# Keys and probabilities in one tile that starts its data 112 bytes up

## The chip, the cores and the metric

The kernel runs on one core of a Trainium2 chip. The metric is the device time of one execution in microseconds (us). Before the change the median of three runs is 1506.08 us (1505.47 to 1506.26). One more execution was profiled; the traces quoted below are of that one.

## The reference

One encoder layer on a sequence of 256 tokens of width 4096, all in float32: a LayerNorm, one wide input projection (4096 to 13,312 columns), two branches that read it, and one output projection with a residual and a second LayerNorm.

```python
p = x @ w_in
y_conv = c_b * centred_short_conv(c_c * c_h, conv_w) * silu(c_z)      # 2048 channels
y_attn = banded_window_attention(a_q, a_k, a_v, sink) * silu(a_z)     # 16 query heads, 4 kv heads, dim 128
y = concatenate([y_conv, y_attn]) @ w_out
return layer_norm(DN_ALPHA * x + y, ln_g, ln_b)
```

The attention of one head takes queries times keys, adds a bias by distance (and masks beyond 128 tokens), makes probabilities with a sink logit in the denominator, and multiplies them with the values.

## The kernel before, in words

Nearly all time is in the two projections. Their weights stream in from memory in pieces of 128 x 2048, and each piece is split into a rounded half `whi` (ScalarE, L204) and a remainder `wlo` (VectorE, L208), so that TensorE can multiply in a reduced float32 form (`F32R`) and still keep float32 accuracy: activations high and low times `whi`, activations high times `wlo`. In a matmul the activations `xT` (or sums of them, `SC`) are the stationary operand, 128 columns; 256 columns of `whi` or `wlo` are the moving operand. Some steps are "pairs" (L257 to L279), which save multiplications by a 7-product scheme, others are plain (L236 to L253, and L909 to L924 for the output projection).

The order of work is written by hand (a manual schedule). A loop (L805 to L829) issues one weight step after another; other work is hung on step numbers with `at(step, function, ...)` and is issued after the step's matmuls on the engines' queues. The input chunks come in the order keys, values, then four times (gate, queries) for the four groups of four heads, then the convolution's chunks. When a group's queries are done, `SPREAD` (L631 to L633) hangs the work of its four heads on the following 32 steps:

- `q_tr`, `q_lo` (L546 to L554): transpose queries into `qhl`, high and low.
- `scores` (L556 to L565): six matmuls, stationary `qhl`, moving `kT` (256 columns). They come at steps 8, 9, 13 and 21 of a group.
- `s_add`, `exps`, `recip`, `norms`: softmax on VectorE and ScalarE.
- `p_tr` (L599 to L607): four transposes of the probabilities on TensorE (128 columns each, at steps 13, 19, 24 and 28), and ScalarE writes the high half of `pT` from their result; `p_lo` (L609) has VectorE write the low half.
- `pv` (L613 to L620): six matmuls, stationary `v`, moving `pT` (256 columns), at steps 19, 22, 28 and 31.
- `out_z` (L622): times the gate, and a store to memory.

So at step 13 the transposes of the first head stand right ahead of the scores of the third, and at steps 19 and 28 a `pv` stands right ahead of the next head's transposes; the other bursts of six have weight matmuls on both sides. Each head has one `scores` and one `pv`: 32 bursts of six in the whole kernel.

`kT` holds the keys of two groups at a time; the keys of the other two are parked in memory through the tile `klate` (which has the place of `pT`, L513) and loaded back by `k_load` (L526) one group later. `v` and `vlate` do the same in the place of `qhl`.

Tiles of a pool lie one after another in each partition, in the order in which they are first named. These are the bytes at which the data of the tiles start, and the remainder by 128:

| tile | role in its matmuls | starts at byte | remainder by 128 |
|---|---|---|---|
| `whi` (3 buffers), `wlo0` to `wlo2` | moving | 82,928; 91,376; 99,824; 132,848; 141,296; 149,744 | 112 |
| `w0`, `w1`, `w2` | moving, in the last step alone | 108,256; 116,448; 124,640 | 96 |
| `kT` | moving | 190,080 | 0 |
| `pT` | moving | 208,512 | 0 |
| `xT` | stationary | 17,280 | 0 |
| `SC` | stationary | 158,336 | 0 |
| `v` | stationary | 194,176 | 0 |
| `qhl` | stationary | 220,800 | 0 |

`whi` and `wlo` have 16 unused bytes ahead of their data (`OFF`, L51, used in `half_tile`, L193 to L200). The last weight step takes its two halves out of the raw buffers `w0` to `w2` instead (L198 to L200), without those 16 bytes; the matmuls that read them are L923 like the others of the output projection.

The pool `pa` holds all attention tiles; when the last head is done it is closed and the pool `pc` opens over the same bytes (`open_pc`, L635).

Of the kernel before, what the change touches and what calls it, by code (L numbers as in the profile page):

```python
# [8 lines left out]
F32 = mybir.dt.float32  # L9
F32R = mybir.dt.float32r  # L10
# [4 lines left out]
P = 128  # L15
D = 4096
S = 256
# [32 lines left out]
N_W = 3  # L50
OFF = 4  # L51
GAP = 64


def units(ci):
# [45 lines left out]
def encoder_kernel(ctx: ExitStack, tc: tile.TileContext, x, emb_g, emb_b, wi, ws, conv_w, sink, wo, ln_g, ln_b, out):  # L101
# [91 lines left out]
    def half_tile(j, name):  # L193
        if j < len(steps) - 1 and name == "whi":
            return wpool.tile([P, PIECE + GAP], F32R, name=name)[:, OFF:OFF + PIECE]
        if j < len(steps) - 1:
# [32 lines left out]
    for name in ("whi", "w0", "w1", "w2", "wlo0", "m", "nm", "wlo1", "den", "es", "wlo2"):  # L229
        n = {"whi": PIECE + GAP}.get(name, PIECE + 2 * OFF if name[:3] == "wlo" else PIECE if name[0] == "w" else 2)  # L230
        wpool.tile([P, n], F32, name=name, bufs={"whi": 3, "m": 4, "nm": 3, "den": 4, "es": 3}.get(name, 1))
# [61 lines left out]
    with tc.tile_pool(name="pro", bufs=1) as pro:  # L293
# [7 lines left out]
        def x_load(i, *cols):  # L301
            for c0, c1 in zip(cols, cols[1:]):
                nc.sync.dma_start(out=xs[i][:, c0:c1], in_=x[i * P:(i + 1) * P, c0:c1])
# [4 lines left out]

        first = [wpool.tile([P, PIECE + GAP], F32, name=f"first{j}", tag="whi")[:, OFF:OFF + PIECE] for j in range(2)]
        x_load(0, 0, 1024, 2048, 3072, 3584, 3840, 4096)  # L310
# [158 lines left out]
    pa = ph.enter_context(tc.tile_pool(name="pa", bufs=1))  # L469
# [15 lines left out]
    def turned(t):  # L485

        return [turned_bank(t, b) for b in range(2)]
# [8 lines left out]
    def halves(hi, lo, src):  # L496
        nc.scalar.activation(hi, src, AF.Copy)
        nc.vector.tensor_tensor(lo, src, hi.bitcast(F32), op=ALU.subtract)

    st_ = {}  # L500
    kT = pa.tile([P, 2, 2, S], F32R, name="kT")
    v = pa.tile([P, 2, 2, 2, P], F32R, name="v")
    kd = dram.tile([P, 2, 2, S], F32, name="kd")
    vd = dram.tile([P, 2, 2, 2, P], F32, name="vd")
# [5 lines left out]

    def k_turn(g):

        late = pa.tile([P, 2, 2, S], F32R, name="klate", tag="pT")  # L513
        for t, ps in zip((kT, late), turned(st_.pop("k"))):
            halves(t[:, :, 0, :], t[:, :, 1, :], ps)
        nc.sync.dma_start(out=kd, in_=late.bitcast(F32))
# [82 lines left out]
    def p_tr(h):  # L599
        p = st_.pop(("p", h))[0]  # L600
        t_ps = ps_att.tile([P, 2, S], F32, name="att")
        for kb in range(2):
            for b in range(2):
                nc.tensor.transpose(t_ps[:, kb, b * P:(b + 1) * P], p[:, b, kb * P:(kb + 1) * P], ident)  # L604
        t = pa.tile([P, 2, 2, S], F32R, name="pT")
        nc.scalar.activation(t[:, 0, :, :], t_ps, AF.Copy)
        st_["pT", h] = t, t_ps  # L607

# [19 lines left out]
    def head(n, *steps):  # L628
        return [(t, f, n) for t, f in zip(steps, (scores, s_add, exps, recip, norms, p_tr, p_lo, pv, out_z))]
# [135 lines left out]
    def chunk_end(j, ci):  # L765
        c0, fn = next((c, f) for c, f in ENDS if IN_ORDER[ci] >= c)
        g = IN_ORDER[ci] - c0
        fn(ci, g)
        if fn is end_k:
            at(j + 1, k_turn, g)  # L770
        if fn is end_cz:
            at(j + 5, s_act)
        if fn is end_z:
            at(j + 5, z_act)
            for b in range(2):
                at(j + 11 + 2 * b, z_tr, g, b) if g else at(j + 8 + b, z_tr, g, b)
        if fn is end_q:
            h = g * GROUP
            for t, f, a in SPREAD:
                at(j + t, f, a if f in (q_tr, q_lo) else h + a)  # L780
            if g < 2:
                at(j + 22, k_load, g)
                at(j + 32, v_load, g)
        if fn in (end_ch, end_cb):
            key, other, tr, mul = ("u", "c", conv_tr, conv_mul) if fn is end_ch else ("g", "s", gate_tr, gate_mul)
            last = ci == len(IN_ORDER) - 1
            if last:
                product(key, other)
            else:
                at(j + (8 if ci == c_ch0 else 4), product, key, other)  # L790
            for t, f, b in ((2, tr, 0), (2, tr, 1), (3, mul, 0), (3, mul, 1)) if last else (
                    (10, tr, 0), (11, tr, 1), (18, mul, 0), (21, mul, 1)) if ci == c_ch0 else (
                            (6, tr, 0), (7, tr, 1), (7, mul, 0), (9, mul, 1)):
                at(j + t, f, g, b)
# [340 lines left out]
```

## Time and profile before

| | |
|---|---|
| median of 3 runs | 1506.08 us |
| the profiled execution's own time | 1505.99 us |
| its span, first to last instruction | 1504.3 us |
| TensorE matmuls busy | 1490.8 us, 99% |
| VectorE busy | 1329.7 us, 88% |
| ScalarE busy | 781.7 us, 52% |
| mean granted TensorE clock | 0.999 |

A busy time is the union of an engine's instructions. Matmuls overlap: each lasts some 0.28 us from start to end, and the next one starts about 0.11 us after it, so the pace of TensorE is read from start to start (or from a long busy stretch divided by its count), not from the length of one.

### The profile page before, as it was taken

The page shows a single profiled execution, that of the slowest core. Times are in us where ns is not written, and L with a number is a line of the kernel's source. Part 1 is how long each engine was busy: PE and PEld are TensorE (multiplying, and loading weights), DVE is VectorE, ACT ScalarE, POOL GpSimd, SP SyncE. Part 2 cuts the span into 40 slices and gives each one's busy share as a digit, 9 for nine tenths or more (in the row PEclk, how much of TensorE's full clock was granted, in tenths as well). Part 3 has the DMA queues.
Part 4 walks back from the last instruction along what each step waited for, and adds up shares of the span by engine and source line. Part 5 has one row for each costly group of instructions (what it writes and reads, how often), then busy time and mean ns, then how long its engine had stood idle before and what let it go on. Part 6 is the DMA issues. An engine that isn't in the chain of part 4 may idle for free.

```text
span 1504.3 us, 30113 instructions
## 1 busy us (share of the span) xinstructions
PE 1490.8 (99%) x12947; PEld 1475.4 (98%) x12947; DVE 1329.7 (88%) x1555; ACT 781.7 (52%) x669; POOL 1.3 (0%) x7
## 2 busy tenths in 40 slices
PE   7999999999999999999999999999999999999998
PEld 4999999999999999999999999999999999999997
DVE  7768989999899998999899999999899688888876
ACT  4545556656566665545555455544556444444431
POOL 0000000000000000000000000000000000000000
PEclk9999999999999999999999999999999999999999
DMA  7555555656555555656556655656557656766673
GB/s 289 217 182 197 210 197 170 208 183 207 196 186 190 181 186 206 233 197 238 187 195 218 220 197 196 220 184 227 205 206 297 261 204 219 261 217 217 219 261 123
DMA packets 71749, 316.18 MB, mean 210 GB/s; under 512 B 8544, under 2 KB 12608, under 8 KB 50880
## 3 DMA queue, kind: packets, MB, share of 16 engines
q1 hardware_dynamic: 70608, 312.43, 58.7%
q8 instruction: 101, 1.65, 0.4%
q10 hardware_dynamic: 1008, 1.84, 0.3%
q14 instruction: 32, 0.26, 0.1%
HBM read 305.23 MB, written 8.91 MB: 209 GB/s over the span
## 4 chain that ended last, share of the span: by engine, by line
PE 98%; DVE 1%; DMA 0%; ACT 0%; SPq 0%; issue 0%; ACTq 0%
PE acc L251 45%; PE acc L923 20%; PE pacc L276 6%; PE pacc L277 6%; PE pacc L279 6%; PE acc L277 4%; PE acc L276 4%; PE acc L279 4%; PE att L493 1%; PE att L618 1%; DVE st L330 0%; PE att L604 0%; PE acc L380 0%; DMA x<-in_x 0%; PE att L363 0%; DVE x L338 0%
## 5 line engine op out<-in xcount | busy, mean ns | idle before, releaser
L204 ACT ACTIVATE whi<-w 128x2048 fp32r<-128x2048 f32 (+1 forms) x354 | 621.7, 1761 | 593.8 <-DVE w L185 231.0
L208 DVE TENSOR_TENSOR wlo<-w,whi 128x2048 fp32r<-128x2048 f32 (+1 forms) x354 | 736.1, 2083 | 102.7 <-ACT whi L204 83.6
L251 PE MATMUL acc<-whi,xT 128*128 128x256 f32 x3952 | 474.0, 276 | 0.0
L251 PEld LDWEIGHTS acc<-whi,xT 128*128 128x128 f32 x3952 | 459.9, 188 | 0.0
L251 PE MATMUL acc<-wlo,xT 128*128 128x256 f32 x1976 | 245.8, 275 | 0.0
L251 PEld LDWEIGHTS acc<-wlo,xT 128*128 128x128 f32 x1976 | 234.0, 188 | 0.0
L923 PE MATMUL acc<-whi,xT 128*128 128x256 f32 x1696 | 201.8, 275 | 0.0
L923 PEld LDWEIGHTS acc<-whi,xT 128*128 128x128 f32 x1696 | 196.6, 188 | 0.4 <-issue 0.4
L183 DVE TENSOR_TENSOR w<-w 128x512 f32<-128x512 f32 x179 | 122.4, 684 | 8.3 <-DMA w<-in_ws 8.3
L923 PE MATMUL acc<-wlo,xT 128*128 128x256 f32 x848 | 105.3, 275 | 0.0
L276 PE MATMUL acc<-whi,xT 128*128 128x256 f32 x370 | 102.1, 276 | 0.0
L277 PE MATMUL acc<-whi,xT 128*128 128x256 f32 x370 | 102.1, 276 | 0.0
L923 PEld LDWEIGHTS acc<-wlo,xT 128*128 128x128 f32 x848 | 100.4, 188 | 0.0
L276 PE MATMUL pacc<-whi,xT 128*128 128x256 f32 x350 | 98.2, 281 | 0.0
L277 PE MATMUL pacc<-whi,xT 128*128 128x256 f32 x350 | 96.5, 276 | 0.0
L279 PE MATMUL pacc<-wlo,xT 128*128 128x256 f32 x350 | 96.2, 275 | 0.0
L279 PE MATMUL acc<-wlo,xT 128*128 128x256 f32 x370 | 92.8, 275 | 0.0
L277 PE MATMUL pacc<-whi,SC 128*128 128x256 f32 x330 | 91.0, 276 | 0.0
L276 PE MATMUL pacc<-whi,SC 128*128 128x256 f32 x330 | 91.0, 276 | 0.0
L279 PE MATMUL pacc<-wlo,SC 128*128 128x256 f32 x330 | 82.9, 275 | 0.0
L184 DVE TENSOR_TENSOR w<-w 128x256 f32<-128x256 f32 x179 | 76.1, 425 | 6.2
L185 DVE TENSOR_TENSOR w<-w 128x256 f32<-128x256 f32 x179 | 76.1, 425 | 6.2
(220 smaller groups left out, 1674.3 us busy)
## 6 DMA issues: line engine op xcount, KB each, us to landing
w<-in_wi SPq DMA_DIRECT2D x112, 1024.0 KB
w<-in_ws SPq DMA_DIRECT2D x202, 512.0 KB
w<-in_wo SPq DMA_DIRECT2D x41, 1024.0 KB
R<-in_wo SPq DMA_DIRECT2D x13, 1024.0 KB
x<-in_x SPq DMA_DIRECT2D x7, 512.0 KB
yl<-yd SPq DMA_DIRECT2D x7, 512.0 KB
xc<-in_x SPq DMA_DIRECT2D x14, 256.0 KB
R<-in_ws SPq DMA_DIRECT2D x6, 512.0 KB
```

The lines of the kernel that those rows point to most:

```text
L183: nc.vector.tensor_tensor(s01, b22, b12.to_broadcast([P, 2, HW]), op=ALU.add)
L184: nc.vector.tensor_tensor(r(6), r(5), r(1), op=ALU.add)
L185: nc.vector.tensor_tensor(r(7), r(6), r(3), op=ALU.add)
L204: nc.scalar.activation(part(j, wh[j]), part(j, raw[j]), AF.Copy)
L208: nc.vector.tensor_tensor(part(j, wl[j]), part(j, raw[j]), part(j, wh[j]).bitcast(F32), op=ALU.subtract)
L251: nc.tensor.matmul(acc[ci, i][:, c:c + HW], x, w[:, k * W + c:k * W + c + HW], start=(first and w is hi and k + off + c == 0), stop=(last ...
L276: nc.tensor.matmul(o, ah, hi[:, w, :], start=(opens and p == 0), stop=False)
L277: nc.tensor.matmul(o, al, hi[:, w, :], start=False, stop=False)
L279: nc.tensor.matmul(o, ah, lo[:, w, :], start=False, stop=(closes and last))
L493: nc.tensor.transpose(ps[:, c, i * P:(i + 1) * P], t[:, i, (2 * b + c) * P:(2 * b + c + 1) * P], ident)
L618: nc.tensor.matmul(o_ps, v[:, g, kb, part_, :], t[:, 0, kb, :], start=(kb + part_ == 0), stop=False)
L923: nc.tensor.matmul(acc[ci, i][:, c:c + HW], y, m[:, k * w + c:k * w + c + HW], start=(first and off + c == 0), stop=(last and c + HW == w))
```

## The change

`kT` and `pT` become two views of one tile `kp` of 8 x 256 + 32 elements (8,320 bytes): `kT` begins 28 elements (112 bytes) up in it, `pT` right behind `kT`. `pT` is no longer allocated anew for each head. An unused tile `gap3` of 128 bytes follows. `kp` starts where `kT` started (190,080), so `kT` starts at 190,192 and `pT` at 194,288, both with remainder 112 by 128. `kp` and `gap3` together take 8,448 bytes in place of 8,192, so `v` starts at 198,528 and `qhl` at 221,056, both still with remainder 0. The instructions, their order and their number are the same. The pool `pc`, which opens later over the same bytes, keeps its addresses.

```diff
 OFF = 4
 GAP = 64
+ATT_OFF = 28
...
     st_ = {}
-    kT = pa.tile([P, 2, 2, S], F32R, name="kT")
+    kp = pa.tile([P, 8 * S + 32], F32R, name="kp")
+    kT, pT = (kp[:, ATT_OFF + 4 * S * k:ATT_OFF + 4 * S * (k + 1)].rearrange("p (a b s) -> p a b s", a=2, b=2) for k in range(2))
+    pa.tile([P, 32], F32, name="gap3")
     v = pa.tile([P, 2, 2, 2, P], F32R, name="v")
...
     def k_turn(g):
 
-        late = pa.tile([P, 2, 2, S], F32R, name="klate", tag="pT")
+        late = pT
         for t, ps in zip((kT, late), turned(st_.pop("k"))):
...
                 nc.tensor.transpose(t_ps[:, kb, b * P:(b + 1) * P], p[:, b, kb * P:(kb + 1) * P], ident)
-        t = pa.tile([P, 2, 2, S], F32R, name="pT")
+        t = pT
         nc.scalar.activation(t[:, 0, :, :], t_ps, AF.Copy)
```

## Prediction

> **What bounds the kernel now.** I read the page first, then the busy times by stretch, then the instructions on the two tiles that move, then the timeline around their matmuls. The page:
>
> ```profile
> span 1504.3 us, 30113 instructions
> PE 1490.8 (99%) x12947; PEld 1475.4 (98%) x12947; DVE 1329.7 (88%) x1555; ACT 781.7 (52%) x669; POOL 1.3 (0%) x7
> ...
> PE 98%; DVE 1%; DMA 0%; ACT 0%; SPq 0%; issue 0%; ACTq 0%
> ```
>
> TensorE is busy for 99% of the span and carries 98% of the chain that ended last. Next, two stretches from the view of busy times by stretch. The heads of all four groups lie in 215 to 595 us; after that come the convolution's chunks and the first part of the output projection.
>
> ```profile
> core 0: us, PE busy (x) PEld busy (x) DVE busy (x) ACT busy (x) POOL busy (x), PEclk, DMA share, GB/s
> 595.00:1200.00 605.00, 605.00 (x5336) 605.00 (x5335) 550.23 (x593) 313.96 (x213) 0.00 (x0) 1.00 0.61 219
> 215.00:595.00 380.00, 380.00 (x3322) 380.00 (x3321) 353.51 (x444) 234.82 (x261) 0.00 (x0) 1.00 0.56 191
> ```
>
> In both, TensorE is busy for the whole stretch at a granted clock of 1.00: it waits for nobody, so time is matmuls times pace. The pace is 605.00/5336 = 113.4 ns from start to start after the heads, and 380.00/3322 = 114.4 ns among them. The difference, 380.00 - 3322 x 0.1134 = 3.3 us, is all that slow pace costs in the heads' stretch, from whatever cause. It is the ceiling of any gain here.
>
> The view by tile gives the matmuls that the change touches (columns: shortest, median and longest duration in ns, first and last start in us):
>
> ```profile
> L563 PE MATMUL att<-kT,qhl x32: 280/283/364, 227.4 to 552.7; 128*128 128x256 f32 x32
> L564 PE MATMUL att<-kT,qhl x32: 281/282/283, 227.5 to 552.8; 128*128 128x256 f32 x32
> L565 PE MATMUL att<-kT,qhl x32: 283/283/283, 227.6 to 552.9; 128*128 128x256 f32 x32
> L527 SPq DMA_DIRECT2D kT<-kd x2: 331/336/342, 276.3 to 368.6; - x2
> ```
> ```profile
> L618 PE MATMUL att<-pT,v x64: 280/282/283, 266.4 to 589.3; 128*128 128x256 f32 x64
> L620 PE MATMUL att<-pT,v x32: 283/283/286, 266.8 to 589.5; 128*128 128x256 f32 x32
> ```
>
> There are 3 x 32 matmuls that move `kT` and 64 + 32 that move `pT`: 192 of 12,947. They move 256 columns, as the weight matmuls do.
>
> **Does the start of the moving operand set the pace?** The trace of before has one place that varies it and little else. On L923 the stationary operand is always `xT`; the moving one is `whi` or `wlo` (remainder 112 by 128) until the last step, which reads `w0` and `w2` (remainder 96). From the timeline of TensorE (start, length from first start to last end, count at the end):
>
> ```profile
> 1472.93 1.98 PE L923 MATMUL acc<-whi,xT 128*128 128x256 f32 x16
> 1474.74 1.07 PE L923 MATMUL acc<-wlo,xT 128*128 128x256 f32 x8
> 1475.65 3.04 PE L923 MATMUL acc<-w,xT 128*128 128x256 f32 x24
> 1478.53 1.98 PE L923 MATMUL acc<-whi,xT 128*128 128x256 f32 x16
> ```
>
> From start to start the 24 matmuls at 112 take 1475.65 - 1472.93 = 2.72 us, 113.3 ns each. The 24 at 96 take 1478.53 - 1475.65 = 2.88 us, 120.0 ns each. Same line, shape, stationary tile and count; only the place of the moving operand differs. The durations say it too (view by source line):
>
> ```profile
> L923 PE MATMUL acc<-whi,xT x1696: 275/275/390, 1147.0 to 1487.0; 128*128 128x256 f32 x189
> ...
> L923 PE MATMUL acc<-w,xT x48: 274/281/384, 1475.7 to 1491.3; 128*128 128x256 f32 x48
> ```
>
> A median of 275 ns at 112, 281 at 96, and 282 to 283 on `kT` and `pT` at 0. Now the attention bursts, in the same view:
>
> ```profile
> 275.41 0.28 PE L563 MATMUL att<-kT,qhl 128*128 128x256 f32 x1
> ...
> 276.12 0.28 PE L276 MATMUL pacc<-whi,xT 128*128 128x256 f32 x1
> ...
> 277.43 0.28 PE L277 MATMUL pacc<-whi,xT 128*128 128x256 f32 x1
> ...
> 278.56 0.64 PE L618 MATMUL att<-pT,v 128*128 128x256 f32 x4
> ...
> 279.27 3.51 PE L251 MATMUL acc<-whi,xT 128*128 128x256 f32 x29
> ```
>
> Six score matmuls take 276.12 - 275.41 = 0.71 us (118 ns each). Then comes what one could miss: the next 11 weight matmuls, which move `whi`, take 277.43 - 276.12 = 1.31 us (119 ns each), and only then are the last ten ahead of `pv` at 278.56 - 277.43 = 1.13 us (113 ns each). The burst costs twice, by its own pace and by a tail behind it. `pv` shows the same: 279.27 - 278.56 = 0.71 us for six, and a tail in the row behind it, as these rows show:
>
> ```profile
> 256.17 3.79 PE L251 MATMUL acc<-whi,xT 128*128 128x256 f32 x32
> ...
> 266.37 0.64 PE L618 MATMUL att<-pT,v 128*128 128x256 f32 x4
> ...
> 267.09 0.60 PE L604 MATMUL att<-ident,p 128*128 128x128 f32 x4
> 267.44 3.93 PE L251 MATMUL acc<-whi,xT 128*128 128x256 f32 x32
> ```
>
> 32 weight matmuls behind other weight matmuls take 3.79 us; 29 of them would take 3.79 - 3 x 0.1134 = 3.45 us, and those at 279.27 took 3.51: 0.06 us of tail. Behind transposes 32 take 3.93 us, 0.14 more: transposes make a tail by themselves, and the change leaves that.
>
> **The sum.** I assume that a burst at remainder 112, entered from the good pace, keeps it, as a change from `whi` to `wlo` or from `xT` to `SC` does, and then leaves no tail.
>
> *Bursts alone.* By the schedule these are 12 scores (steps 8, 9, 21) and 8 `pv` (steps 22, 31). A score burst with its tail takes 0.71 + 1.31 = 2.02 us for 17 steps; at 113.4 ns it is 1.93; 0.09 us is won. A `pv` wins 0.71 - 0.68 + 0.06 = 0.09 us. 20 x 0.09 = 1.8 us.
>
> *`pv` ahead of transposes* (steps 19, 28; 8 of them). Six take 267.09 - 266.37 = 0.72 us against 0.68: 0.04 us each, 0.3 us. The tail is the transposes' and stays.
>
> *Scores behind transposes* (step 13; 4 of them):
>
> ```profile
> 247.84 0.36 PE L563 MATMUL att<-kT,qhl 128*128 128x256 f32 x1
> ...
> 248.63 0.28 PE L276 MATMUL pacc<-whi,xT 128*128 128x256 f32 x1
> ...
> 249.94 0.28 PE L277 MATMUL pacc<-whi,xT 128*128 128x256 f32 x1
> ```
>
> From 247.84 to 249.94 are 17 steps in 2.10 us, 0.17 over the good pace. Behind transposes the good operand, too, pays 0.14 us (the row at 267.44), so 0.03 us each is won, 0.1 us.
>
> Together, with the terms unrounded, 1.11 + 0.72 + 0.32 + 0.13 = 2.3 us. The lower bound, if the tails stay, is the bursts' own 20 x 0.03 + 8 x 0.04 = 0.9 us; the upper one is the 3.3 us above. I take 2.3 because the rows of the tail itself carry it.
>
> *What else moves, at nothing.* No instruction is added, and every queue, SP's and POOL's among them, holds the same instructions in the same order. Writes to `pT` now start at remainder 112. For VectorE and ScalarE the nearest rows are the splits, which write there already; the same excerpt has the writes to `pT`:
>
> ```profile
> 273.52 2.29 DVE L208 TENSOR_TENSOR wlo<-w,whi 128x2048 fp32r<-128x2048 f32 x1
> 274.81 1.92 ACT L204 ACTIVATE whi<-w 128x2048 fp32r<-128x2048 f32 x1 [0.53 <-PE pacc L277]
> ...
> 275.73 0.69 DVE L611 TENSOR_TENSOR pT<-att,pT 128x512 fp32r<-128x512 f32 x1
> ```
> ```profile
> 248.48 0.58 ACT L606 ACTIVATE pT<-att 128x512 fp32r<-128x512 f32 x1
> ```
>
> Per 512 columns the splits take 0.57 and 0.48 us, and the writes to `pT` 0.69 and 0.58 with their fixed part, so nothing says that 112 is slower; 16 writes on each engine could lose or win hundredths of a microsecond, beside VectorE's 380.00 - 353.51 = 26 us of idle time and ScalarE's 145 us. The two loads of keys (issued at 276.3 and 368.6) fill the half of `kT` that the same group has just finished with and that is next read two groups on; if the odd start made them slower by some microseconds, a group's length of about 92 us (368.6 - 276.3) covers it. The pool that opens over these bytes finds other tiles beneath: `tm` now lies over a probability tile and the gate tile `z`, not over `pT`. The last read of `z` and the first write of `tm`:
>
> ```profile
> 594.57 1.22 DVE L694 TENSOR_TENSOR w<-q,z 128x1024 f32<-128x1024 f32 x1
> ```
> ```profile
> 603.37 0.38 ACT L672 ACTIVATE tm<-pacc 128x256 f32<-128x256 f32 x1
> ```
>
> 7.6 us lie between them; were that cover gone, ScalarE would wait and TensorE only after it.
>
> **The rivals.** *Own pace only.* The tails come from the switch of operands and stay; the gain is 0.9 to 1.1 us, 1505.1. For it: transposes leave a tail too. Against: the 24 matmuls at 96, slow as they are, leave none (the row at 1478.53 has the clean 1.98 us), so a tail is not a toll on every switch.
>
> *The place does not matter.* The pace comes from the stationary tiles `qhl` and `v`, or from what the other engines do in those moments; time stays at 1506.1. Against it stands the pair at 1472.93 and 1475.65. For it: that pair compares 96 with 112, and no row has `kT` or `pT` at 112. In the Trainium skill, "TensorE: Matmul & The Clock Gate" (Part 2, first step of what happens when a matmul is issued) says that the streaming operand and the weights come through two independent read ports and that loading the next weights takes no bandwidth from the running matmul; its section on the back-to-back issue gap makes the gap a matter of the number of columns alone, by an estimate from it 256/2.4 + 2.5 = 109 ns wherever the operand lies. By that rule the change is worth nothing, and the trace's 113.3 against 120.0 ns at one line does not agree with it.
>
> *Slower: one tile, one lock.* If waits were drawn for the tile as a whole, scores would wait for writes to `pT`, though they read only keys. The scores at 247.84 stand behind the copy that ends at 248.48 + 0.58 = 249.06, 1.22 us later; those at 275.41 stand behind the write that ends at 275.73 + 0.69 = 276.42, 1.01 us later. TensorE executes in order, so the weight matmuls queued behind would wait too. Four groups x 2.23 = 8.9 us, less 2.3: 1512.7. It decides from 2.3/4 = 0.6 us of waiting a group. Against it:
>
> ```profile
> 31.25 0.69 DVE L385 CAST xT<-hT 128x1024 fp32r<-128x1024 f32 x1
> ...
> 31.65 1.55 PE L251 MATMUL acc<-whi,xT 128*128 128x256 f32 x11
> ```
>
> The matmuls at 31.65 read columns 8 to 11 of the tile `xT` while VectorE writes columns 12 to 15 of it, a write that the program issues ahead of them (L425 to L429): waits go by the part of a tile, not by the tile.
>
> *More than counted.* Slow matmuls that I leave to the transposes go too; at the ceiling of 3.3 us, 1502.8. Only the ceiling speaks for it: nothing in the change touches the transposes.
>
> **How the numbers follow.** The profiled execution took 1505.99 us around its span of 1504.3, 0.1 us from the median of 1506.08, so the sum is taken from the median as it is: 1506.08 - 2.3 = 1503.8 us. A span of 1502.0 us should go with it. Chances: the forecast 0.72, own pace only 0.09, place without effect 0.10, one lock 0.04, more than counted 0.05. The range takes in the first three and leaves out the last two: from 1503.0 (the forecast less 0.8, for the spread of the three runs, 1505.47 to 1506.26) to 1506.1 (no effect). 0.2% is 3.0 us, about what a measurement of this kernel can tell from no change. Faster by more than that needs 1503.07 or less: the last case and the lower edge of the first, 0.08. Slower by more than that is the lock alone, 0.04. The rest, 0.88, is within 0.2%: I forecast a gain of 0.15% that is real in the trace and small in the clock.
>
> **What would show it right or wrong.** If each step holds, the profile after has medians of about 275 ns, as `whi` on L923 has, on L564 and L565, L618 and L620, where 282 and 283 stood; a lone burst of six takes 0.68 us to the start of the next matmul, and the weight matmuls behind it go at 113 ns from the first; behind the four scores at step 13 a tail of some five matmuls remains; behind transposes 32 matmuls still take 3.93 us; the stretch of 380 us holds some 20 matmuls more (2.3/0.1134). If the six are fast and the eleven behind them slow, own pace only was right. If the six still take 0.71, the place does not matter. The forecast is wrong on the other side if TensorE has idle time on L563 or L618, with ScalarE's L606 or VectorE's L611 named as what ended it, or if the writes on those lines grow so long that they outlast their cover.

## The result

The changed kernel takes 1503.45 us (median of 22 runs, 1503.02 to 1503.81); the kernel before, run beside it, 1505.95 us (22 runs, 1505.33 to 1506.35). That is 2.50 us less; the ratio is 0.9984, 95% interval 0.9978 to 0.9990, a small gain but clear of the noise. The forecast was 1503.8 us, 2.3 us less.

The page of the changed kernel (lines below the first line of the new tile are numbered three higher than before, or one higher where only the new constant lies above them):

```profile
span 1501.7 us, 30113 instructions
PE 1488.7 (99%) x12947; PEld 1473.4 (98%) x12947; DVE 1329.3 (89%) x1555; ACT 782.0 (52%) x669; POOL 1.3 (0%) x7
...
PE 98%; DVE 1%; DMA 0%; ACT 0%; SPq 0%; issue 0%; ACTq 0%
```

The span is 2.6 us shorter, TensorE's busy time 2.1 us, and the number of instructions is the same: the same work at a better pace. The busy times by stretch (same columns as before) say where:

```profile
595.00:1200.00 605.00, 605.00 (x5335) 605.00 (x5335) 550.24 (x594) 315.16 (x213) 0.00 (x0) 1.00 0.62 218
215.00:595.00 380.00, 380.00 (x3345) 380.00 (x3344) 355.63 (x445) 235.58 (x262) 0.00 (x0) 1.00 0.57 194
```

After the heads the pace is what it was (5335 matmuls where 5336 stood). Among the heads 3345 fit where 3322 did: 23 more, 23 x 0.1134 = 2.6 us, the whole difference. The view by tile, for the shared tile:

```profile
L621 PE MATMUL att<-kp,v x64: 275/275/275, 266.0 to 586.7; 128*128 128x256 f32 x64
...
L566 PE MATMUL att<-kp,qhl x32: 275/275/363, 227.3 to 550.3; 128*128 128x256 f32 x32
...
L567 PE MATMUL att<-kp,qhl x32: 275/275/282, 227.4 to 550.4; 128*128 128x256 f32 x32
...
L568 PE MATMUL att<-kp,qhl x32: 275/275/282, 227.5 to 550.5; 128*128 128x256 f32 x32
...
L623 PE MATMUL att<-kp,v x32: 275/275/281, 266.4 to 586.9; 128*128 128x256 f32 x32
L609 ACT ACTIVATE kp<-att x16: 568/580/599, 248.2 to 579.5; 128x512 fp32r<-128x512 f32 x16
L614 DVE TENSOR_TENSOR kp<-att,kp x16: 680/683/684, 254.3 to 585.6; 128x512 fp32r<-128x512 f32 x16
...
L530 SPq DMA_DIRECT2D kp<-kd x2: 407/412/416, 275.9 to 367.5; - x2
```

All five medians are 275 ns where 282 and 283 stood. The writes to the probabilities are as long as before (580 ns on ScalarE and 683 ns on VectorE, 582 and 684 before). The two loads of keys take SP longer to issue, 412 ns in place of 336, and nobody waits for it. The start of the tile is not the reason: in two runs below with the keys at the same start, e4 and e12, they take 350 and 348 ns. The timeline of TensorE around the places that the prediction used:

```profile
265.99 0.61 PE L621 MATMUL att<-kp,v 128*128 128x256 f32 x4
...
266.67 0.60 PE L607 MATMUL att<-ident,p 128*128 128x128 f32 x4
267.03 3.92 PE L252 MATMUL acc<-whi,xT 128*128 128x256 f32 x32
...
274.98 0.28 PE L566 MATMUL att<-kp,qhl 128*128 128x256 f32 x1
...
275.66 0.28 PE L277 MATMUL pacc<-whi,xT 128*128 128x256 f32 x1
...
278.04 0.61 PE L621 MATMUL att<-kp,v 128*128 128x256 f32 x4
...
278.72 0.50 PE L252 MATMUL acc<-whi,xT 128*128 128x256 f32 x3
```

Six score matmuls take 275.66 - 274.98 = 0.68 us. The 21 weight matmuls behind them take 278.04 - 275.66 = 2.38 us, 113.3 ns each: there is no tail. The products with the values take 278.72 - 278.04 = 0.68 us. Behind transposes, at 267.03, the tail stands as before (3.92 us, 3.93 before).

### The profile page after: what moved, and what is told of

Its sections match the earlier page's. It is cut to its first block, busy times and chain, and to the rows that moved or that the text cites. A ratio compares the mean times of both kernels' runs of the same rounds, so it can differ in the third digit from the quotient of the medians.

```text
span 1501.7 us, 30113 instructions
## 1 busy us (share of the span) xinstructions
PE 1488.7 (99%) x12947; PEld 1473.4 (98%) x12947; DVE 1329.3 (89%) x1555; ACT 782.0 (52%) x669; POOL 1.3 (0%) x7
## 3 DMA queue, kind: packets, MB, share of 16 engines
q10 hardware_dynamic: 1008, 1.84, 0.3%
## 4 chain that ended last, share of the span: by engine, by line
PE 98%; DVE 1%; DMA 0%; ACT 0%; SPq 0%; issue 0%; ACTq 0%
PE acc L252 45%; PE acc L926 20%; PE pacc L278 6%; PE pacc L277 6%; PE pacc L280 6%; PE acc L278 4%; PE acc L277 4%; PE acc L280 4%; PE att L494 1%; DVE st L331 0%; PE att L621 0%; PE att L607 0%; PE acc L381 0%; DMA x<-in_x 0%; PE att L364 0%; DVE x L339 0%
```

## The experiments

Two numbers are read from each trace. *Burst* is the time from the start of a lone burst of six to the start of the weight matmul behind it, *tail* what the slow weight matmuls behind it take over 113.4 ns each. Both are means over the 12 lone score bursts and the 8 lone products with the values, from the start times of the instructions in the trace; the excerpts show one burst of each at 10 ns. Times are against the kernel before on the same chip. Their intervals are some 0.09% (1.3 us) wide to each side, so by the times alone only the changed kernel, e2 and e11 are told from the kernel before. The traces, in which bursts of one kind agree to a nanosecond or two, carry the verdicts.

The theory at first was that of the prediction: the start of the moving operand, by its remainder by 128, sets the pace. The rivals were that the sharing of one tile or the other tiles' new places did it, and later that the distance between moving and stationary operand does. This is what all runs gave. Starts are remainders by 256, which turned out to be needed; the pair is moving | stationary.

| run | scores: starts | burst, tail ns | products: starts | burst, tail ns | time less before, us |
|---|---|---|---|---|---|
| before | 128 \| 128 | 714, 58 | 128 \| 128 | 714, 58 | |
| changed | 240 \| 128 | 680, 0 | 240 \| 128 | 680, 0 | -2.50 |
| e1 | 128 \| 128 | 714, 58 | 128 \| 128 | 714, 58 | -0.04 |
| e2 | 240 \| 128 | 680, 0 | 0 \| 128 | 702, 31 | -2.05 |
| e4 | 240 \| 128 | 680, 0 | 240 \| 112 | 720, 43 | -0.95 |
| e5 | 128 \| 16 | 722, 60 | 128 \| 144 | 709, 54 | -0.26 |
| e6 | 144 \| 128 | 711, 22 | 192 \| 128 | 707, 0 | -1.53 (one run) |
| e7 | 176 \| 128 | 710, 49 | 224 \| 128 | 720, 0 | -0.64 (one run) |
| e8 | 160 \| 128 | 700, 53 | 208 \| 128 | 719, 60 | -0.50 (one run) |
| e10 | 112 \| 128 | 704, 35 | 112 \| 128 | 704, 36 | -0.99 (one run) |
| e12 | 240 \| 0 | 704, 61 | 240 \| 0 | 704, 61 | -0.23 |
| e9 | 112 \| 128 | 704, 61 | 112 \| 128 | 704, 61 | -0.64 (one run) |
| e13 | 16 \| 160 | 704, 32 | 16 \| 160 | 704, 32 | -0.89 |
| e11 | 240 \| 128 | 680, 0 | 240 \| 128 | 680, 0 | -3.03 |

**e1: the shared tile without the 112 bytes.**

```diff
-ATT_OFF = 28
+ATT_OFF = 0
```

> The shared tile, the gap behind it and all other tiles stay as in the changed kernel; only the 112 bytes ahead of the keys are gone, so keys and probabilities both move from remainder 0 by 128. Place theory (the start of the moving operand sets the pace): all of the gain is lost; time within 0.4 us of the kernel before, a lone burst of six 0.71 us to the next matmul, a tail of 11 slow matmuls behind it, medians 282 to 283 ns on the six lines. Sharing theory (the gain comes from one tile for both, or from the new places of values, probabilities and queries): the gain of 2.5 us stays, medians 275 ns.

1505.84 us against 1505.88; ratio 0.9999 (0.9991 to 1.0008). Its timeline:

```profile
275.38 0.28 PE L566 MATMUL att<-kp,qhl 128*128 128x256 f32 x1
...
276.09 0.28 PE L277 MATMUL pacc<-whi,xT 128*128 128x256 f32 x1
...
277.40 0.28 PE L278 MATMUL pacc<-whi,xT 128*128 128x256 f32 x1
```

0.71 us for the burst, 1.31 for the eleven behind it, to the hundredth what stood before the change. The sharing theory falls: without the 112 bytes, one tile for both, the gap and the new places of the other tiles are worth nothing.

**e2: keys at 112, probabilities not.**

```diff
-    kT, pT = (kp[:, ATT_OFF + 4 * S * k:ATT_OFF + 4 * S * (k + 1)].rearrange(...) for k in range(2))
+    kT, pT = (kp[:, o:o + 4 * S].rearrange(...) for o in (ATT_OFF, 4 * S + 32))
```

> Keys at remainder 112, probabilities at remainder 0, all else as changed. Place theory: the parts add up. The scores win 12 x 0.092 + 4 x 0.03 = 1.2 us, the products with the values nothing; time 1.2 us under the kernel before; medians 275 ns on the scores' lines, 282 to 283 on the others, and a tail only behind the latter. Rival (the gain needs the whole attention at 112, because one slow burst puts the next out of step): under 0.6 us won and scores slow too.

1503.83 us against 1505.88; ratio 0.9987 (0.9978 to 0.9996):

```profile
274.96 0.28 PE L566 MATMUL att<-kp,qhl 128*128 128x256 f32 x1
...
275.64 0.28 PE L277 MATMUL pacc<-whi,xT 128*128 128x256 f32 x1
...
278.02 0.63 PE L621 MATMUL att<-kp,v 128*128 128x256 f32 x4
...
278.72 2.01 PE L252 MATMUL acc<-whi,xT 128*128 128x256 f32 x16
```

The scores came out as expected (0.68 us, no tail), but the whole won 2.05 us, not 1.2: the products took 0.70 us and had half a tail. That is some 0.4 us. Another 0.3 us lies in the 35 bursts of transposes that stand apart from scores and products, whose operands this run leaves in place; no theory here accounts for it. The products' remainder by 128 was 0 as before. By 256 it was not: the probabilities began at 194,304, remainder 0, where 128 stood. So 128 is too coarse a measure, and the place theory needed mending.

**e4: the values at 112 too.**

```diff
-    pa.tile([P, 32], F32, name="gap3")
-    v = pa.tile([P, 2, 2, 2, P], F32R, name="v")
+    v = pa.tile([P, 8 * P + 32], F32R, name="v")[:, ATT_OFF:ATT_OFF + 8 * P].rearrange(...)
```

> Keys and probabilities at 112 as changed, and the stationary values moved from remainder 0 to 112 as well; queries stay at 0. Place theory (only the moving operand counts): nothing changes, 113 ns from start to start in both bursts, time as the changed kernel within 0.4 us. Relation theory (what counts is the distance between the starts of the moving and the stationary operand): the products with the values go back to 118 to 120 ns and get their tail again, 1.0 us of the gain lost; the scores stay at 113.

1504.93 us against 1505.88; ratio 0.9993 (0.9984 to 1.0002):

```profile
275.25 0.28 PE L565 MATMUL att<-kp,qhl 128*128 128x256 f32 x1
...
275.94 0.28 PE L277 MATMUL pacc<-whi,xT 128*128 128x256 f32 x1
...
278.32 0.64 PE L620 MATMUL att<-kp,v 128*128 128x256 f32 x4
...
279.04 1.68 PE L252 MATMUL acc<-whi,xT 128*128 128x256 f32 x13
```

The moving probabilities are where the changed kernel has them, and their matmuls take 279.04 - 278.32 = 0.72 us with a tail; the scores, whose queries did not move, stay good. So the place theory falls in its plain form: the stationary operand's start counts too. The run lost 1.5 us of the gain where 1.0 was expected: a product ahead of transposes, with these and their tail, takes 1236 ns, more than the 1211 of the kernel before.

**e5: the same distance, another place.** Keys and probabilities back at 128, queries and values 16 bytes up in their tiles.

```diff
+    v = pa.tile([P, 8 * P + 32], F32R, name="v")[:, 4:4 + 8 * P].rearrange(...)
...
+        q = st_["qhl"] = pa.tile([P, 4 * S + 32], F32R, name="qhl")[:, 4:4 + 4 * S].rearrange(...)
```

> Keys and probabilities at remainder 0 as in the kernel before, the stationary queries and values at remainder 16, so that the distance of moving to stationary is the same 112 (by 128) as in the changed kernel. Place theory: nothing won, 118 to 120 ns and tails in both bursts, time within 0.4 us of the kernel before. Relation theory: the whole gain of 2.5 us, 113 ns in both.

1505.62 us against 1505.88; ratio 0.9998 (0.9989 to 1.0008):

```profile
275.44 0.29 PE L566 MATMUL att<-kp,qhl 128*128 128x256 f32 x1
...
276.16 0.28 PE L278 MATMUL pacc<-whi,xT 128*128 128x256 f32 x1
```

0.72 us. The distance of 112 (for the scores by 256 as well: 128 less 16) is not enough either: the six steps of a score burst, from start to start, are 122, 121, 119, 121, 119 and 121 ns, with no return to 113.

**e6, e7, e8, e10: other starts of the moving operand**, with the stationary ones at 128. e6 to e8 differ from e2 in the two offsets alone: `(4, 4 * S + 16)`, `(12, 4 * S + 24)` and `(8, 4 * S + 20)`, in elements of 4 bytes. e10 has `ATT_OFF = 60` in a tile of `8 * S + 64` and no `gap3`.

> Keys 16 bytes and probabilities 64 bytes above remainder 0 by 128, stationary tiles at 0, all else as changed. If only 112 is good (the last 16 bytes ahead of a 128-byte line): both bursts take 0.70 to 0.72 us and have tails. If every start that is 16 bytes off a multiple of 32 is good: scores 0.68 us and no tail, the products with the values slow. If every start but 0 is good: both 0.68 us, the whole gain of 2.5 us.

> Keys at remainder 48, probabilities at remainder 96, else as changed. Only 112 good: both slow (96 was 120 ns a matmul on the last step of the kernel before). Odd multiples of 16 good: scores 0.68 us, products with the values 0.72. Every start but 0 good: both 0.68.

> Keys at remainder 32, probabilities at remainder 80, else as changed. Only 112 good: both slow. Odd multiples of 16 good: scores 0.70 to 0.72 us with tails, products with the values 0.68 without. Every start but 0 good: both 0.68.

> Keys and probabilities 240 bytes up in their tile in place of 112: the same remainder by 128, the other one by 256. If the remainder by 128 decides: as the changed kernel, 0.68 us a burst, no tail, 2.5 us under the kernel before. If the remainder by 256 decides (with keys alone at 112 the probabilities lay at 0 by 256 and not at 128 as before, and their bursts took 702 ns, not 714): bursts of 0.70 us or more, tails, and at least 1 us of the gain lost.

None of the six starts in e6 to e8 is good: bursts of 700 to 720 ns. Of all starts beside a stationary 128, only the changed kernel's 112 by 128 is good, and not every start with that remainder: e10 (1504.77 us in its one run, 1505.76 before) has 112 by 256, takes 0.70 us and has a tail. Of the ten starts tried, only 240 is good.

```profile
275.22 0.28 PE L565 MATMUL att<-kp,qhl 128*128 128x256 f32 x1
...
275.92 0.28 PE L277 MATMUL pacc<-whi,xT 128*128 128x256 f32 x1
```

The same runs show that a slow burst need not have a tail: at 192 and at 224 (e6, e7) the products take 707 and 720 ns and the weight matmuls behind them are at full pace at once, as behind the last step's `w0` and `w2`. For e7:

```profile
278.43 0.64 PE L621 MATMUL att<-kp,v 128*128 128x256 f32 x4
...
279.15 3.79 PE L252 MATMUL acc<-whi,xT 128*128 128x256 f32 x32
```

The six take 0.72 us, and the 32 behind them the clean 3.79. So a tail does not follow from a slow burst alone, and the two parts of the sum have to be read separately. The steps inside this burst (117, 125, 116, 123, 118, 121 ns) are, within a nanosecond, those that the 24 matmuls on `w0` and `w2` repeat in the kernel before, whose pair is also 224 | 128: the same pair gives the same pattern on another line.

**e12: without the gap.** `gap3` is dropped, which moves queries and values from 128 to 0 by 256 and leaves every remainder by 128.

> The changed kernel without the unused 128 bytes behind the shared tile: moving starts stay at 240 by 256, the stationary queries and values (and the probabilities and gates that the transposes load) go from 128 to 0 by 256; by 128 all remainders stay. If the remainders by 128 decide on the stationary side: as the changed kernel, 680 ns a burst and no tail, 2.5 us under the kernel before. If it is the pair by 256: bursts of 0.70 us or more with tails, at least 1 us of the gain lost.

1505.83 us against 1506.06; ratio 0.9999 (0.9990 to 1.0008):

```profile
275.30 0.28 PE L565 MATMUL att<-kp,qhl 128*128 128x256 f32 x1
...
276.00 0.28 PE L277 MATMUL pacc<-whi,xT 128*128 128x256 f32 x1
```

Nearly all of the gain is gone. The unused 128 bytes, which look like padding, are needed as much as the 112.

**e9: nearly everything 128 bytes higher.** The identity's tile grows by 128 bytes and `gap3` is dropped, so weight halves are at 112 and activations at 0 by 256.

```diff
-    ident = const.tile([P, P], F32, name="ident")
+    ident = const.tile([P, P + 32], F32, name="ident")[:, 0:P]
...
-    pa.tile([P, 32], F32, name="gap3")
```

> All tiles behind the identity lie 128 bytes higher (weights halves from 240 to 112 by 256, activations from 128 to 0), except values and queries, which stay at 128 by 256 since the unused gap ahead of them is dropped; keys and probabilities go to 112. If what counts is the distance of moving to stationary by 256: the weight matmuls stay at 113.4 ns (distance 112 as before), and only the attention bursts slow down (distance 240), time 1505 to 1506 us. If the place itself by 256 counts (a moving start at 112 by 256 took 704 ns a burst and not 680 when the stationary was at 128): all 12,000 weight matmuls go at 116 to 120 ns, 30 to 80 us more than before.

1505.42 us in its one run, 1506.06 before:

```profile
256.04 3.79 PE L252 MATMUL acc<-whi,xT 128*128 128x256 f32 x32
...
275.29 0.28 PE L565 MATMUL att<-kp,qhl 128*128 128x256 f32 x1
...
276.00 0.28 PE L277 MATMUL pacc<-whi,xT 128*128 128x256 f32 x1
...
1475.30 3.04 PE L925 MATMUL acc<-w,xT 128*128 128x256 f32 x24
1478.17 1.98 PE L925 MATMUL acc<-whi,xT 128*128 128x256 f32 x16
```

The weight matmuls, now 112 | 0, take the same 3.79 us for 32 as at 240 | 128, while the attention at 112 | 128 takes 0.71 (704 ns in the mean). So it is neither the one start nor the other but the two together: 112 | 0 and 240 | 128 are good, 112 | 128 and 240 | 0 are not in bursts of six. Pairs that differ by 128 in both starts behave alike: the two good ones, the two bad ones (704 ns with a tail of 61, here and in e12), and those of the last step, where the 24 matmuls on `w0` and `w2` are at 96 | 0 here and at 224 | 128 in the kernel before and take 120 ns each in both.

**e13: both up by 32.** `ATT_OFF = 36` and a tile of `8 * S + 40` put keys and probabilities at 16 and queries and values at 160 by 256: the good distance once more, now with a stationary start that is a multiple of 32. (The expectation calls e5's shift 16; counted from the changed kernel it was 144, which is 16 by 128.)

> Keys and probabilities at 16 by 256 and queries and values at 160 by 256: moving and stationary tiles of the attention both 32 bytes higher than in the changed kernel, their distance still 112; the weight matmuls as before. Distance theory (moving minus stationary by 256 must be 112): 680 ns a burst and no tail, 2 to 2.5 us under the kernel before. Place theory (fast only where the stationary starts at a multiple of 128; moving both by 16 from 240 and 128 to 128 and 16 in an earlier run, also at distance 112 for the scores, gave 722 ns): 0.70 us a burst or more, with tails, under 1.3 us won.

1505.10 us against 1505.99; ratio 0.9994 (0.9984 to 1.0004):

```profile
275.20 0.28 PE L566 MATMUL att<-kp,qhl 128*128 128x256 f32 x1
...
275.90 0.28 PE L277 MATMUL pacc<-whi,xT 128*128 128x256 f32 x1
```

Slow again, so the distance theory finds no support. But this run does not end it. The six steps are 118, 114, 120, 119, 116 and 117 ns. Behind transposes, where the matmuls of the changed kernel come back to their pace, the steps are 118, 119, 114, 120, 119, 116, 117, 121, 119 and then 113: the same sequence without its second step. So the burst at 16 | 160 may be slow by itself, or only too short to come back from the switch of places. What stands against the distance is e5, whose scores show no such return.

**e11: the identity matrix at 240.** The transposes move the identity, which starts at 128 by 256. Here it starts at 240; some small tiles change places so that all other moving and stationary tiles keep their starts.

```diff
-    ident = const.tile([P, P], F32, name="ident")
+    ident = const.tile([P, P + ATT_OFF], F32, name="ident")[:, ATT_OFF:ATT_OFF + P]
...
-    cw = const.tile([P, CONV_T, 3], F32, name="cw")
+    cw = small.tile([P, CONV_T, 3], F32, name="cw", bufs=1)
...
```

> The changed kernel with the identity matrix, which the transposes move, from 128 to 240 by 256; a few small tiles change places so that every other moving and stationary tile keeps its start. Place theory: the tail behind transposes (130 ns behind each of 47 bursts, some 60 of it in ten slow matmuls at 119 ns) comes from the identity's start and goes like that of the attention bursts: 47 x 0.06 = 2.8 us less than the changed kernel. Rival: the tail comes from the gap that the switch between transposes and matmuls leaves (a step of 201 ns), and nothing changes, within 0.4 us of the changed kernel.

1503.03 us (1502.93 to 1503.19) against 1506.06; ratio 0.9980 (0.9971 to 0.9989):

```profile
266.72 0.60 PE L604 MATMUL att<-ident,p 128*128 128x128 f32 x4
267.07 3.90 PE L250 MATMUL acc<-whi,xT 128*128 128x256 f32 x32
```

It is the best version measured, 3.0 us under the kernel before, but some 0.4 us better than the changed kernel and not 2.8; the intervals of the two ratios overlap. The tail behind transposes is 3.90 - 3.79 = 0.11 us here and 0.13 in the changed kernel. The rival was nearer: nearly all of that tail stays. Nor are the 0.4 us shown to be the identity's. They lie in the bursts of transposes with their tails, the 35 others (0.3 us less than in the changed kernel) and the eight behind products (0.16 us); in e6, with the identity at 128, the same two groups are as much shorter.

## Why the prediction was right, and where its reason was too simple

**The sum.** The terms came out close to what was worked out. From the start times of both traces, a lone burst with its tail went from 714 + 58 to 680 ns: 20 x 0.092 = 1.84 us (forecast 1.11 + 0.72). Products ahead of transposes, transposes and tail included, went from 1072 + 139 to 1043 + 130 ns: 8 x 0.038 = 0.30 us (0.32). Transposes ahead of scores went from 1157 + 58 to 1149 + 19: 4 x 0.047 = 0.19 us (0.13). The 35 other bursts of transposes gave some 0.06 us, which was not forecast. Together 2.4 us, beside 2.5 in the medians and 2.6 in the spans. To take the tail as a term of its own made the forecast: the bursts' own pace was 0.9 us of it.

**The marks in the profile.** Medians of 275 ns, 0.68 us a burst, no tail behind lone bursts: all there. Behind the scores at step 13 a tail of four matmuls (116, 117, 121, 119 ns in the trace) where "some five" was said; with the six scores ahead of them they make the same ten steps, within a nanosecond, as weight matmuls right behind transposes, so the scores now run as weight matmuls do. 3.92 us behind transposes, 3.93 said. 23 matmuls more in the stretch, some 20 said. A span of 1501.7 us, 1502.0 said. No wait on L566 or L621: "one tile, one lock" did not come.

**The reason.** The step "does the start of the moving operand set the pace" compared 96 with 112 at one stationary tile and concluded on the moving operand by its remainder by 128. For this change that was enough, because it puts keys and probabilities at 240 by 256 and leaves queries and values at 128, the very pair of the weight matmuls. As a reason it was wrong twice: remainders by 256 count (e2, e10, e12), and the stationary operand's start counts beside the moving one's (e4, e12). As far as its reason goes, the size of the gain was luck: by remainders of 128 neither 240 in place of 112 nor the gap would matter, and e10 and e12, which change just these, lose 1.5 us (in its one run) and 2.3 us of the gain. "The place does not matter", held for 1 in 10, was wrong, but its own argument, that the stationary tiles play a part, was half right.

In the Trainium skill, "TensorE: Matmul & The Clock Gate" (Part 2, first step) has the weight load take nothing from the running matmul, through a read port of its own. These runs do not agree that the two are independent for this kind of matmul: of what TensorE reads, e12 moves nothing but stationary tiles by 128 bytes, and the burst goes from 680 to 704 ns, while beside a moving start of 112 a stationary start of 0 is good (e9). Its section on the back-to-back issue gap gives the gap by the number of columns, with weight loads and without, and knows no part of the operands' places; here the gap at 256 columns is 113 to 120 ns by the operands' places. The prediction's estimate of 109 ns is by its formula for a lone matmul; for matmuls with a weight load each the section has 81 ns at 128 columns and 131 ns at 512.

**What stays open.** Why 112 past the stationary start is good was not settled: 15 pairs in the attention and four in the weight matmuls were seen, and no trace shows what makes a pair slow. Nor do bursts of six show how each pair would go in a long run. In the attention every good burst has the starts of the weight matmuls around it, and every slow one has others, so "the same places as the neighbours" would fit the attention as well as "a good pair". The last step shows that a pair can be slow by itself: its 24 matmuls repeat the same six steps and never come back to 113 ns. That the neighbours count as well is seen at 112 | 128, which takes 704 ns in e9 and in e10, beside weight matmuls at different places, with tails of 61 and 35 ns. And the 35 other bursts of transposes with their tails are some 0.3 us shorter than before in e2, e5, e6 and e8, but 0.06 in the changed kernel; what sets that is open too.

## What to carry to other kernels

Where TensorE is the bound and each matmul has its own weight load, read the pace from start to start for every line and compare lines of one shape; a group that is 5% slower may only lie in another place. Copy the pair of starts, moving and stationary, from the fast group, here as remainders by 256 bytes, and keep the padding that holds the stationary tiles in place. These runs show it for `F32R` matmuls of 256 columns alone. Look at the instructions behind a slow burst as well as at the burst: here more than half of what it cost stood on innocent lines.

## What the runs showed of the hardware

- An `F32R` matmul of 256 columns with a weight load each goes at 113.4 ns from start to start where moving and stationary operands start at 240 and 128, or at 112 and 0, by 256 bytes. At the other pairs tried, bursts of six between weight matmuls take 700 to 722 ns, 117 to 120 ns each; 24 in a row at 224 and 128, or at 96 and 0, take 120 ns each.
- The slow pace can outlast its cause: in the kernel before, the 11 weight matmuls behind a slow burst go at 115 to 122 ns, 58 ns together over the good pace, and then the pace drops back by itself. In the other runs the tail of a slow burst between weight matmuls is of none to 12 matmuls, 0 to 61 ns. Behind four transposes of the changed kernel, the last of which the next matmul follows after 28 ns, come a step of some 200 ns and nine of 114 to 121 ns.
- Writes of VectorE and ScalarE to a tile that starts 112 bytes past a multiple of 128 take what they took at 0 (683 and 580 ns for 128 x 512, 684 and 582 before).
